# Seven products per group: three of them accumulate in one bank, two banks are copied into banks, and two sums between banks stand where there were four

## The chip, the cores and the metric

The kernel runs on one core of a Trainium2 chip. Five engines work side by side, each through its own queue in order: TensorE (PE, matrix products; PEld is its loading of the stationary operand), VectorE (DVE), ScalarE (ACT), GpSimd (POOL) and SyncE (SP, which here only issues transfers). Products are written to banks of PSUM; one bank holds 128 rows of 512 float32 numbers. The metric is the time of the whole program on the device in microseconds (us), as the median of the runs; smaller is better.

## The reference

One decoder block on 256 rows of width 2048 in float32. The two feed-forward parts, which the change touches, are these:

```
h = h + 0.5 * swiglu(rms_norm(h, ffn1_norm), ffn1_w_gu, ffn1_w_down)
h = h + hybrid_mixer(rms_norm(h, mix_norm), ...)
h = h + 0.5 * swiglu(rms_norm(h, ffn2_norm), ffn2_w_gu, ffn2_w_down)
gate = sigmoid(rms_norm(h, ple_norm) @ ple_w_gate)
h = h + gate * (p @ ple_w_proj)
return rms_norm(h, final_norm)

def swiglu(x, w_gu, w_down):
    gate, up = split(x @ w_gu, 2)          # 2048 -> 2 x 5632
    return (silu(gate) * up) @ w_down      # 5632 -> 2048
```

## The kernel before

**Precision.** Each float32 operand is split into a rounded part and a rest (`hi` and `lo`, for weights `whi`/`wlo`, for activations `nTh`/`nTl` and `hTh`/`hTl`), and each product is three matmuls: hi·hi, hi·lo, lo·hi. ACT makes the rounded part of a weight (line 74), DVE the rest (line 75). A weight pair is 256 rows of a weight by 512 columns; for both halves of the 256 rows of x it takes 12 matmuls of 128x512.

**Groups.** A feed-forward part is a list of groups (`Group`, line 245). A group makes 256 rows by two blocks of 512 columns, so it owns four banks: c11 and c21 (first block of columns, rows 0 to 127 and 128 to 255) and c12 and c22 (second block). In the profile they carry the names g, g, u, u in a group of the gate and up product and d, d, d, d in a group of the down product. Groups take turns between two pools of four banks. `PARTS` cuts the 11 blocks of the hidden width into parts of 3, 4 and 4: the gate and up groups of a part come first, then its two down groups.

**Seven products.** A share of each group's depth (`ns` pairs of each block; 4 for gate and up, 2 or 3 for down) is not multiplied plainly in eight block products but in seven, in the manner of Strassen and Winograd: sums of blocks of the activations (`halves`, lines 420 to 462: `S`, split into `Sh` and `Sl`) are multiplied with sums of blocks of the weights (`all_sums`, lines 287 to 322: `R`, split by ACT into `shi`, line 295, and by DVE into `slo`, line 296). `product(i)` (line 324) issues product i: 3·ns matmuls, so 12, 9 or 6. There are 32 such groups, 15 in the first feed-forward part, 16 in the second and one behind it, so 224 products. The first one or two groups of a feed-forward part have no such products, and the first group that has them is marked `first`.

Before the change product 0 goes to c11, 1 to c12, 2 to c21, 3 to c22. After product 2, `add` (line 338) adds c11 to c21 and subtracts c21 from c12; after product 3 it subtracts c22 from c21 and adds c12 to c22. Each `add` is an ACT copy of one bank to a buffer in SBUF (`part`, line 341) and a DVE sum of the other bank with it (line 342). Products 4, 5 and 6 are accumulated on c11, c12 and c21.

**Order.** `plan` (line 351) strews the seven products of the next group between the plain pairs of the current one, one product behind each pair, from the second or third pair on; where the pairs run out, two products stand side by side. `next_weights` (line 82) loads and splits weights up to two pairs and one sum ahead. The code is written in that order, but a scheduler in the layer below sets the final order of each engine's queue: it may move an instruction past others on its engine. So the place of a product, a copy or a sum in its queue is read from the built program, not from the code.

Twice in the kernel a down group needs the hidden values of the gate and up group just ahead of it. They travel from DVE through DRAM back to a tile `tT` and are split by ACT (line 499, `hTh`) and DVE (line 500, `hTl`).

Of the kernel before, what the change touches and what calls it, by code (L numbers as in the profile page):

```python
# [13 lines left out]
ALU = mybir.AluOpType  # L14
# [29 lines left out]
def block_kernel(ctx, tc, a, out):  # L44
    nc = tc.nc
# [18 lines left out]
    def weight_pair(src, pool=wp, bufs=3, parts=1):  # L64

        raw = wp.tile([P, 2, NB], F32, tag="raw", name="raw", bufs=4)
        hi = pool.tile([P, 2, NB], F32R, tag="whi", name="whi", bufs=bufs)
        lo = pool.tile([P, 2, NB], F32R, tag="wlo", name="wlo", bufs=bufs)
        for i in range(parts):
            j = slice(2 * i // parts, 2 * (i + 1) // parts)  # L70
            nc.sync.dma_start(out=raw[:, j, :], in_=src[:, j, :])
        for i in range(parts):
            j = slice(2 * i // parts, 2 * (i + 1) // parts)
            nc.scalar.copy(hi[:, j, :], raw[:, j, :])  # L74
            nc.vector.tensor_tensor(out=lo[:, j, :], in0=raw[:, j, :], in1=hi[:, j, :], op=ALU.subtract)  # L75
        return hi, lo
# [5 lines left out]
    def next_weights():  # L82

        ahead = max(1, min(LEAD, done[1] // 2))
        while done[0] < len(order):
            kind, src = order[done[0]]
            if kind != "load" and sum(k == kind for k, _ in split) > (ahead if kind == "pair" else 1):
                break
            done[0] += 1
            if kind == "load":  # L90
                src()
            elif kind == "sum":
                split.append((kind, next(src.sums)))
            else:
                split.append((kind, weight_pair(src, parts=2 if not done[1] and not split else 1)))
        done[1] += 1
        return split.pop(0)[1]
# [145 lines left out]
    current, sides = [None], {}  # L243

    class Group:
# [78 lines left out]
        def product(self, i):  # L324

            if i == 0:
                self.new_banks()
            c11, c21, c12, c22 = self.banks
            out = (c11, c12, c21, c22, c11, c12, c21)[i]
            whi, wlo = next_weights()  # L330
            for g in range(self.ns):
                xh, xl = sides[self.kind](i, g)
                st, sp = i < 4 and g == 0, i < 4 and g == self.ns - 1
                nc.tensor.matmul(out, xh, whi[:, g, :], start=st, stop=False, skip_group_check=True)  # L334
                nc.tensor.matmul(out, xh, wlo[:, g, :], start=False, stop=False, skip_group_check=True)  # L335
                nc.tensor.matmul(out, xl, whi[:, g, :], start=False, stop=sp, skip_group_check=True)  # L336

            def add(out, x, op):

                part = act.tile([P, NB], F32, tag="nat", name="part", bufs=4)  # L340
                nc.scalar.copy(part, x)
                nc.vector.tensor_tensor(out=out, in0=out, in1=part, op=op)

            if i == 2:
                add(c21, c11, ALU.add)
                add(c12, c21, ALU.subtract)
            elif i == 3:
                add(c21, c22, ALU.subtract)
                add(c22, c12, ALU.add)

    def plan(n):

# [67 lines left out]
    def halves(kind, his, los, ns, wait=0):  # L420


        for _ in range(wait):
            yield
        fp = current[0]

        sh = fp.tile([P, NS, 2, 2, P], F32R, tag="Sh", name="Sh")
        sl = fp.tile([P, NS, 2, 2, P], F32R, tag="Sl", name="Sl")

        def side(i, g):  # L430
            if i in (0, 4, 6):
                k, t = 2 * (g % 2) + (i > 0), i // 6
                c = slice(t * P, (t + 1) * P)
                return his[g // 2][:, k, c], los[g // 2][:, k, c]
            j, t = {1: (1, 1), 2: (0, 0), 3: (0, 1), 5: (1, 0)}[i]
            return sh[:, g, j, t, :], sl[:, g, j, t, :]

        sides[kind] = side

        for g0 in range(0, ns, 2):  # L440
            n = min(2, ns - g0)
            hi, lo = his[g0 // 2], los[g0 // 2]
            keep = lambda ins: ins
            if g0 and n == 1:

                keep = tc.keep_in_program_order
                yield
            if n == 2:
                x = fp.tile([P, 2 * NB], F32, tag="sil", name="S")
            else:  # L450
                x = act.tile([P, NB], F32, tag="nat", name="S", bufs=4)
            keep(nc.vector.tensor_tensor(out=x, in0=hi[:, 0:2 * n].bitcast(F32).rearrange("p k x -> p (k x)"),
                                         in1=lo[:, 0:2 * n].bitcast(F32).rearrange("p k x -> p (k x)"), op=ALU.add))
            xv = x.rearrange("p (g j t y) -> p g j t y", g=n, j=2, t=2)
            a11, a12, a21, a22 = (xv[:, :, j, t, :] for t in range(2) for j in range(2))
            for o, y, z, op in ((a22, a21, a22, ALU.subtract), (a21, a21, a11, ALU.subtract),
                                (a11, a22, a11, ALU.subtract), (a12, a11, a12, ALU.add)):
                nc.vector.tensor_tensor(out=o, in0=y, in1=z, op=op)
            sx = [y[:, g0:g0 + n].rearrange("p g j t y -> p (g j t y)") for y in (sh, sl)]
            nc.scalar.copy(sx[0], x)  # L460
            nc.vector.tensor_tensor(out=sx[1], in0=x, in1=sx[0], op=ALU.subtract)
            yield

    def ffn(n, nT, r, scale, next_norm, stat):
        xs = picker(*nT)
        late = callable(r)
        with tc.tile_pool(name="ffn", bufs=1) as fp:
# [40 lines left out]
            nxt = None  # L508
            current[0] = fp
            lanes.add(1, halves("gu", *nT, NS, 6 if late else 0))  # L510
            for group, todo in ffn_plan[n]:
                if group.kind == "behind":
# [4 lines left out]
                if dn and group.nb and not group.last:  # L517
                    lanes.add(1, halves("gu", *nT, NS))
                elif dn and group.nb and group.follower:
                    lanes.add(1, halves("behind", *nxt, NS_BEHIND, 4))  # L520
                elif not dn and group.follower.kind == "dn":
                    lanes.add(1, halves("dn", hTh[i0:], hTl[i0:], NS_DOWN[group.part]))
# [116 lines left out]
    with tc.tile_pool(name="fin", bufs=1) as fp:  # L639
# [35 lines left out]
        for _, (nb, g) in todo:  # L675
            whi, wlo = next_weights()
            for j in range(2):
                k = 2 * g + j
                xh, xl = xs(k)
                for t in range(2):  # L680
                    c = slice(t * P, (t + 1) * P)
                    gt, sp = group.banks[2 * nb + t], k == KD - 1
# [695 lines left out]
```

## Time and profile before

| | |
|---|---|
| median of 3 runs | 1946.12 us (1945.83 to 1947.10) |
| the profiled execution: span from its first to its last instruction | 1944.1 us |
| PE busy, TensorE clock granted | 99% of the span, 0.999 |
| DVE, ACT, POOL busy | 82%, 60%, 8% |
| mean of a product's ACT copy and DVE sum (lines 341, 342) | 0.584 to 0.591 us, 0.693 to 0.696 us |
| first feed-forward part, mixer, second part | to about 690 us, to about 1155 us, to about 1850 us |

The median lies 2.0 us above the span of the profiled execution. In the rows below, a row of the timeline is: start, length, engine, line, operation, output from input, number of instructions merged in the row, and in brackets the idle time of the engine just before it with what ended that. A row of the windows is: the stretch, its length, and for PE, PEld, DVE, ACT and POOL the busy time with the number of instructions in brackets, then the granted TensorE clock, the busy share of the DMA engines and GB/s. A matmul's row is longer than its place in the pipeline: what counts is the distance between two starts.

### The profile page before, as it was taken

To read this page: it belongs to the slowest core of one execution; us is meant where nothing else is said; L and a number is where in the kernel's file an instruction comes from. 1 tells how busy PE (TensorE), PEld (TensorE's weight loads), DVE (VectorE), ACT (ScalarE), POOL (GpSimd) and SP (SyncE) were. 2 spreads that over 40 slices of the span, in tenths; PEclk is the share of its full clock that TensorE was granted. 3 is DMA by queue.
4 is the path that set the end of the run, shared out by engine and by line. 5 is a ranking of instruction groups with operands and counts; after the bars stand their busy time and mean duration, and the time that the engine had idled before them with its cause. 6 is when DMAs were issued, how large, how long until landed. Compare 5 with 4: busy or idle time off the path is not lost.

```text
span 1944.1 us, 24295 instructions
## 1 busy us (share of the span) xinstructions
PE 1927.9 (99%) x8882; PEld 1593.1 (82%) x8882; DVE 1603.2 (82%) x1743; ACT 1163.4 (60%) x1358; POOL 148.8 (8%) x226
## 2 busy tenths in 40 slices
PE   9999999999999999999999999999999999999998
PEld 7888888888888888878788888888888888888887
DVE  7879988998889866797856679899888998889965
ACT  6655656566665567654555456566565755657654
POOL 0010110000001000010100000011000100001000
PEclk9999999999999999999999999999999999999999
DMA  8778898898898765556464776788898988989864
GB/s 306 269 217 291 256 292 272 248 296 247 269 288 255 224 218 171 173 167 218 159 215 157 243 278 229 236 268 285 260 278 253 306 257 261 264 263 273 253 212 147
DMA packets 144183, 475.06 MB, mean 244 GB/s; under 512 B 19648, under 2 KB 47296, under 8 KB 129856
## 3 DMA queue, kind: packets, MB, share of 16 engines
q1 hardware_dynamic: 104896, 293.78, 43.6%
q0 software_dynamic: 25920, 160.44, 29.9%
q10 hardware_dynamic: 13248, 19.30, 3.3%
q8 instruction: 69, 1.13, 0.2%
q14 instruction: 50, 0.41, 0.1%
HBM read 451.44 MB, written 22.02 MB: 244 GB/s over the span
## 4 chain that ended last, share of the span: by engine, by line
PE 91%; DVE 6%; issue 1%; DMA 1%; ACT 1%; POOL 0%; SPq 0%; POOLq 0%; DVEq 0%; ACTq 0%
PE d L540 5%; PE d L541 5%; PE d L542 5%; PE u L541 5%; PE u L542 5%; PE u L540 5%; PE g L541 4%; PE g L542 4%; PE pj L109 4%; PE pj L110 4%; PE pj L111 4%; PE g L540 4%; PE g L335 4%; PE g L334 4%; PE g L336 4%; PE u L334 3%
## 5 line engine op out<-in xcount | busy, mean ns | idle before, releaser
L74 ACT CAST whi<-raw 128x1024 fp32r<-128x1024 f32 (+1 forms) x489 | 511.7, 1050 | 420.0 <-PE pj L111 108.9
L75 DVE TENSOR_TENSOR wlo<-raw,whi 128x1024 fp32r<-128x1024 f32 (+1 forms) x489 | 590.8, 1217 | 155.8 <-ACT whi L74 153.1
L296 DVE TENSOR_TENSOR slo<-R,shi 128x2048 fp32r<-128x2048 f32 (+2 forms) x224 | 444.4, 1987 | 99.9 <-ACT shi L295 99.7
L295 ACT CAST shi<-R 128x2048 fp32r<-128x2048 f32 (+2 forms) x224 | 374.0, 1673 | 185.6 <-DVE R L304 74.4
L109 PE MATMUL pj<-whi,nTh 128*128 128x512 f32 x448 | 179.4, 401 | 0.0
L110 PE MATMUL pj<-wlo,nTh 128*128 128x512 f32 x448 | 175.3, 391 | 1.4 <-DVE wlo L75 1.4
L111 PE MATMUL pj<-whi,nTl 128*128 128x512 f32 x448 | 174.9, 390 | 0.0
L541 PE MATMUL d<-wlo,hTh 128*128 128x512 f32 x448 | 174.4, 389 | 0.0
L542 PE MATMUL d<-whi,hTl 128*128 128x512 f32 x448 | 174.0, 389 | 0.0
L540 PE MATMUL d<-whi,hTh 128*128 128x512 f32 x448 | 173.1, 390 | 0.0
L541 PE MATMUL g<-wlo,nTh 128*128 128x512 f32 x400 | 156.1, 390 | 0.6 <-DVE wlo L75 0.6
L540 PE MATMUL g<-whi,nTh 128*128 128x512 f32 x400 | 154.9, 390 | 1.2 <-ACT whi L74 0.9
L542 PE MATMUL g<-whi,nTl 128*128 128x512 f32 x400 | 155.9, 390 | 0.0
L541 PE MATMUL u<-wlo,nTh 128*128 128x512 f32 x400 | 155.7, 389 | 0.1
L542 PE MATMUL u<-whi,nTl 128*128 128x512 f32 x400 | 155.6, 389 | 0.0
L540 PE MATMUL u<-whi,nTh 128*128 128x512 f32 x400 | 154.2, 389 | 0.0
L304 DVE TENSOR_TENSOR R<-R 128x2048 f32<-128x2048 f32 (+2 forms) x68 | 135.4, 1991 | 0.1
L110 PEld LDWEIGHTS pj<-wlo,nTh 128*128 128x128 f32 x448 | 84.2, 188 | 19.2 <-DVE wlo L75 3.0
L540 PEld LDWEIGHTS d<-whi,hTh 128*128 128x128 f32 x448 | 84.1, 188 | 17.9 <-ACT hTh L499 0.7
L542 PEld LDWEIGHTS d<-whi,hTl 128*128 128x128 f32 x448 | 84.1, 188 | 17.7
L111 PEld LDWEIGHTS pj<-whi,nTl 128*128 128x128 f32 x448 | 84.1, 188 | 17.5
L541 PEld LDWEIGHTS d<-wlo,hTh 128*128 128x128 f32 x448 | 84.1, 188 | 17.4
(327 smaller groups left out, 3482.5 us busy)
## 6 DMA issues: line engine op xcount, KB each, us to landing
raw<-in_w_gu SPq DMA_DIRECT2D x199, 512.0 KB, 5.7
raw<-in_w_down SPq DMA_DIRECT2D x112, 512.0 KB, 6.4
raw<-in_w_in SPq DMA_DIRECT2D x112, 512.0 KB, 3.4
R<-in_w_gu2q POOLq DMA_DIRECT2D x54, 1024.0 KB, 8.1
R<-in_w_gu1q POOLq DMA_DIRECT2D x48, 1024.0 KB, 8.7
raw<-in_w_out SPq DMA_DIRECT2D x32, 512.0 KB, 4.4
R<-in_w_down11q POOLq DMA_DIRECT2D x12, 768.0 KB, 6.8
R<-in_w_down12q POOLq DMA_DIRECT2D x12, 768.0 KB, 6.3
```

The source lines that it names most:

```text
L74: nc.scalar.copy(hi[:, j, :], raw[:, j, :])
L75: nc.vector.tensor_tensor(out=lo[:, j, :], in0=raw[:, j, :], in1=hi[:, j, :], op=ALU.subtract)
L109: nc.tensor.matmul(outs[t], xh[:, c], whi[:, j, :], start=st, stop=False)
L110: nc.tensor.matmul(outs[t], xh[:, c], wlo[:, j, :], start=False, stop=False)
L111: nc.tensor.matmul(outs[t], xl[:, c], whi[:, j, :], start=False, stop=sp)
L295: keep(nc.scalar.copy(hi, w))
L296: nc.vector.tensor_tensor(out=lo, in0=w, in1=hi, op=ALU.subtract)
L304: keep(nc.vector.tensor_tensor(out=self.raw[x], in0=self.raw[x], in1=self.raw[y], op=ALU.add))
L334: nc.tensor.matmul(out, xh, whi[:, g, :], start=st, stop=False, skip_group_check=True)
L540: nc.tensor.matmul(out, xh[:, c], whi[:, j, :], start=st, stop=False, skip_group_check=True)
L541: nc.tensor.matmul(out, xh[:, c], wlo[:, j, :], start=False, stop=False, skip_group_check=True)
L542: nc.tensor.matmul(out, xl[:, c], whi[:, j, :], start=False, stop=sp, skip_group_check=True)
```

## The change

```
-            out = (c11, c12, c21, c22, c11, c12, c21)[i]
+            out = (c21, c12, c21, c21, c11, c12, c21)[i]
             whi, wlo = next_weights()
+            if i == 0 and self.first == "2":
+
+                for x in (c11, c22):
+                    nc.tensor.matmul(x, sides[self.kind](0, 0)[0], whi[:, 0, :], start=True, stop=True,
+                                     skip_group_check=True)
             for g in range(self.ns):
                 xh, xl = sides[self.kind](i, g)
-                st, sp = i < 4 and g == 0, i < 4 and g == self.ns - 1
+                st, sp = i < 2 and g == 0, i < 4 and g == self.ns - 1
...
-            def add(out, x, op):
-
+            if i < 2:
+                nc.scalar.copy((c11, c22)[i], out)
+            elif i < 4:
                 part = act.tile([P, NB], F32, tag="nat", name="part", bufs=4)
-                nc.scalar.copy(part, x)
-                nc.vector.tensor_tensor(out=out, in0=out, in1=part, op=op)
-
-            if i == 2:
-                add(c21, c11, ALU.add)
-                add(c12, c21, ALU.subtract)
-            elif i == 3:
-                add(c21, c22, ALU.subtract)
-                add(c22, c12, ALU.add)
+                nc.scalar.copy(part, c21)
+                x = (c12, c22)[i - 2]
+                nc.vector.tensor_tensor(out=x, in0=x, in1=part, op=ALU.subtract)
...
-            for o, y, z, op in ((a22, a21, a22, ALU.subtract), (a21, a21, a11, ALU.subtract),
+            for o, y, z, op in ((a22, a21, a22, ALU.subtract), (a21, a11, a21, ALU.subtract),
```

Product 0 now goes to c21, and ACT copies c21 into the bank c11; product 1 goes to c12 as before, and ACT copies it into the bank c22. Products 2 and 3 are accumulated on c21 by PE itself; after each of them ACT copies c21 to `part`, and DVE subtracts that from c12 after product 2 and from c22 after product 3. One sum of the activations changes its sign. So each group keeps four ACT copies, of which two now write a bank, and has two DVE sums in place of four. In the first such group of the second feed-forward part, two matmuls on c11 and c22 are added. The lines behind the change move down by five: `shi`, `slo` and the sums keep theirs, the products' matmuls are lines 339 to 341 (334 to 336 before), the copies between banks line 344, the copies to `part` line 347, and the sums line 349.

The queues move with it at a few places. In the rows below, the operand names carry the buffer numbers, which differ between the two programs; the first bank in the list of a group is c11, then c21, c12, c22.

On PE, in the first seven-product group of the first feed-forward part (banks g0_722, g1_723, u0_724, u1_725), where the last matmul of product 0 stands between plain matmuls of the group ahead. Before:

```order
L336 MATMUL g0_722<-shi_660,nTl_104 128x512
L334 MATMUL u0_724<-shi_684,Sh_295 128x512
L335 MATMUL u0_724<-slo_685,Sh_295 128x512
L336 MATMUL u0_724<-shi_684,Sl_296 128x512
L541 MATMUL g0_524<-wlo_579,nTh_101 128x512
```

The same place now:

```order
L341 MATMUL g1_723<-shi_660,nTl_104 128x512
L541 MATMUL g0_524<-wlo_579,nTh_101 128x512
L542 MATMUL g0_524<-whi_578,nTl_105 128x512
L541 MATMUL g1_525<-wlo_579,nTh_101 128x512
L542 MATMUL g1_525<-whi_578,nTl_105 128x512
```

Before, three matmuls of product 1 stood here, and its other nine (three, then six) among the next plain pairs; now all twelve stand behind six plain pairs, 70 matmuls further on, and the plain matmuls that need the weight rests `wlo_579`, and a pair later `wlo_597`, move up by three and by six places.

On PE, in the second down group behind the first three hidden blocks of the first feed-forward part (banks d0_1315, d1_1316, d0_1317, d1_1318 before; d0_1307, d1_1308, d0_1309, d1_1310 now), at products 2 and 3, just ahead of the plain matmuls that need the late hidden values `hTh_1238` (now `hTh_1230`). Before:

```order
L334 MATMUL d1_1316<-shi_1325,Sh_1012 128x512
L334 MATMUL d1_1318<-shi_1354,Sh_1012 128x512
L335 MATMUL d1_1316<-slo_1326,Sh_1012 128x512
L336 MATMUL d1_1316<-shi_1325,Sl_1013 128x512
L334 MATMUL d1_1316<-shi_1325,Sh_1012 128x512
L335 MATMUL d1_1316<-slo_1326,Sh_1012 128x512
L336 MATMUL d1_1316<-shi_1325,Sl_1013 128x512
L335 MATMUL d1_1318<-slo_1355,Sh_1012 128x512
```

Now:

```order
L339 MATMUL d1_1308<-shi_1318,Sh_1008 128x512
L340 MATMUL d1_1308<-slo_1319,Sh_1008 128x512
L341 MATMUL d1_1308<-shi_1318,Sl_1009 128x512
L339 MATMUL d1_1308<-shi_1318,Sh_1008 128x512
L340 MATMUL d1_1308<-slo_1319,Sh_1008 128x512
L341 MATMUL d1_1308<-shi_1318,Sl_1009 128x512
L339 MATMUL d1_1308<-shi_1348,Sh_1008 128x512
L340 MATMUL d1_1308<-slo_1349,Sh_1008 128x512
```

Products 2 and 3 went to two banks (c21 and c22) and were interleaved; now product 3 follows product 2 in one bank with no matmul between. The mirror of this group in the second feed-forward part stands in the same way.

On ACT at that same place. Before:

```order
L295 CAST shi_1325<-R_1150 128x1024
L295 CAST shi_1354<-R_1208 128x1024
L74 CAST whi_1399<-raw_1398 128x1024
L295 CAST shi_1392<-R_1218 128x1024
L499 CAST hTh_1238<-tT_1310 128x4x4x32 x2
L341 COPY part_1389<-d1_1316 128x512
```

Now:

```order
L295 CAST shi_1318<-R_1145 128x1024
L344 COPY d1_1310<-d0_1309 128x512
L295 CAST shi_1348<-R_1200 128x1024
L74 CAST whi_1390<-raw_1389 128x1024
L347 COPY part_1380<-d1_1308 128x512
L295 CAST shi_1383<-R_1210 128x1024
L499 CAST hTh_1230<-tT_1302 128x4x4x32 x2
```

The copy between banks (after product 1) and the copy of product 2 now stand ahead of the weight sum of product 4 (`shi_1383`) and of the split of the hidden values. The mixer between the two feed-forward parts has the same rows in the same order on every engine.

## The prediction, made before the changed kernel was run

> **What bounds the kernel now.** I read the page's busy times and its chain of work first.
>
> ```profile
> PE 1927.9 (99%) x8882; PEld 1593.1 (82%) x8882; DVE 1603.2 (82%) x1743; ACT 1163.4 (60%) x1358; POOL 148.8 (8%) x226
> ...
> PE 91%; DVE 6%; issue 1%; DMA 1%; ACT 1%; POOL 0%; SPq 0%; POOLq 0%; DVEq 0%; ACTq 0%
> ```
>
> PE carries the chain. DVE, where the change takes work away, holds 6% of it: short spells in which PE stands ready for something that DVE has just finished. How long PE really stood there is in the waits of PE (total us, times, longest):
>
> ```profile
> PE pj L110 <- DVE wlo L75: 1.4, 3, 0.6
> PE vp L1109 <- DVE R L1130: 1.2, 1, 1.2
> ...
> PE d L335 <- DVE slo L296: 0.6, 2, 0.3
> PE u L335 <- DVE slo L296: 0.3, 1, 0.3
> ```
>
> The longest belong to the mixer, which the change leaves alone. In the feed-forward parts they are fractions of a microsecond. But a matmul's row overlaps the next, so a stall is longer than the idle time shown; it is the starts that count. The windows show where starts are missing:
>
> ```profile
> 50.00:100.00 50.00, 49.30 (x217) 40.07 (x216) 43.49 (x34) 31.09 (x31) 1.30 (x2) 1.00 0.74 267
> 150.00:200.00 50.00, 49.70 (x216) 40.00 (x216) 49.23 (x52) 30.83 (x31) 5.74 (x8) 1.00 0.87 278
> 250.00:300.00 50.00, 50.00 (x222) 41.38 (x222) 40.52 (x29) 31.20 (x27) 5.05 (x8) 1.00 0.89 285
> 1300.00:1350.00 50.00, 49.70 (x216) 39.81 (x215) 48.85 (x49) 31.44 (x31) 5.34 (x8) 1.00 0.90 290
> ```
>
> Undisturbed, PE starts 222 matmuls in 50 us, one each 0.225 us, at the full granted clock (1.00). It lacks 5 in the stretch from 50 us and 6 each in those from 150 and 1300 us. These three stretches are the stalls that the change can take away or make longer; the last two are also where DVE is busy 98% of the time.
>
> **The change part by part.**
>
> Removed: half of the DVE sums. The copies and sums of before, by line (count, then shortest, median and longest in ns):
>
> ```profile
> L341 ACT COPY part<-d x48: 567/583/599, 131.3 to 1791.7; 128x512 f32<-128x512 f32 x48
> L341 ACT COPY part<-g x40: 569/588/593, 82.1 to 1833.7; 128x512 f32<-128x512 f32 x40
> L341 ACT COPY part<-u x40: 589/591/602, 96.3 to 1837.3; 128x512 f32<-128x512 f32 x40
> ```
>
> ```profile
> L342 DVE TENSOR_TENSOR d<-d,part x48: 689/693/700, 133.1 to 1792.3; 128x512 f32<-128x512 f32 x48
> L342 DVE TENSOR_TENSOR g<-g,part x40: 691/693/700, 91.0 to 1838.2; 128x512 f32<-128x512 f32 x40
> L342 DVE TENSOR_TENSOR u<-u,part x40: 687/690/700, 95.0 to 1838.8; 128x512 f32<-128x512 f32 x40
> ```
>
> There are 128 of each, four in each of 32 groups. 64 sums of 0.69 us go, 44 us of DVE's 1603. As PE is busy 99%, this is worth only what it takes off PE's stalls; elsewhere DVE idles longer.
>
> Changed in kind: 64 of the 128 ACT copies now write a bank. The trace has no ACT write to a bank. Of ACT's rows that read a bank and write a buffer, the nearest is the copy itself, 0.584 us; an activation of the same shape is slower and one of half its width the shortest of that kind:
>
> ```profile
> L505 ACT ACTIVATE sil<-g,rstd 128x512 f32<-128x512 f32 x44 | 28.9, 687 | 10.5 <-DVE Sl L461 8.5 <-PE g L542 1.5
> ...
> L936 ACT ACTIVATE cT<-tr_p,conv 128x256 f32<-128x256 f32 x24 | 10.2, 470 | 9.0 <-DVE cT L938 9.0
> ```
>
> I bound it by 0.47 and 0.69 us and take 0.58. Between the two bounds, 64 copies differ by 14 us on an engine that idles 780. The next matmul that touches a copied bank is product 2 on c21 and product 4 on c11, with at least a plain pair and product 1 between (24 matmuls, 5.4 us), so either bound costs nothing on PE.
>
> Added: two matmuls in the second part, straight onto PE: 2 x 0.225 = **+0.45 us**.
>
> Moved: product 1 in the first group of the first part. Here are PE and then DVE at that place before:
>
> ```profile
> 65.11 0.39 PE L336 MATMUL g<-shi,nTl 128*128 128x512 f32 x1
> 65.34 0.40 PE L334 MATMUL u<-shi,Sh 128*128 128x512 f32 x1
> 66.04 0.50 PE L335 MATMUL u<-slo,Sh 128*128 128x512 f32 x1 [0.30 <-DVE slo L296]
> 66.38 0.39 PE L336 MATMUL u<-shi,Sl 128*128 128x512 f32 x1
> 67.17 0.50 PE L541 MATMUL g<-wlo,nTh 128*128 128x512 f32 x1 [0.40 <-DVE wlo L75]
> 67.51 0.40 PE L542 MATMUL g<-whi,nTl 128*128 128x512 f32 x1
> ```
>
> ```profile
> 63.70 2.29 DVE L296 TENSOR_TENSOR slo<-R,shi 128x2048 fp32r<-128x2048 f32 x1
> 65.90 1.22 DVE L75 TENSOR_TENSOR wlo<-raw,whi 128x1024 fp32r<-128x1024 f32 x1
> 67.04 2.29 DVE L304 TENSOR_TENSOR R<-R 128x2048 f32<-128x2048 f32 x1
> 69.24 3.49 DVE L75 TENSOR_TENSOR wlo<-raw,whi 128x1024 fp32r<-128x1024 f32 x3
> ```
>
> PE waits twice: for `slo` (0.47 us late, then 0.11 until it is back in step) and for `wlo` (0.57 and 0.11), 1.26 in all. The three matmuls of product 1 that filled part of the gap are now gone from it, and DVE's order here is unchanged, since the first sums that the change removes come at 91 us. So the plain matmul due at 65.34 waits until 67.17 for the same `wlo`: 1.83 + 0.11. The next plain pair follows after 12 matmuls rather than 15: due at 67.51 + 11 x 0.225 = 69.99, while its `wlo`, the first of the three from 69.24, is ready at 70.46 and usable some 0.05 later (as 67.17 follows 67.12): 0.52 + 0.11. Together 2.57, so **+1.31 us**. Before, that pair was due three matmuls later, at 67.51 + 14 x 0.225 = 70.66, and did not wait. The two `wlo` after that are ready at 71.6 and 72.8, ahead of need. Product 1 itself moves 16 us down, where its `slo` is long ready; nothing is won there, since it waited only as filler.
>
> A new wait: product 3 now needs c21, and so the ACT copy behind product 2. Queued behind it on PE are plain matmuls; on ACT, behind the copy that waits for PE, the next `shi` and `whi`. From the start of product 2's last matmul: 0.39 for its row, 0.58 for the copy, and about 0.05 for each hand-over, 1.07 us. In nearly all groups a plain pair of 12 matmuls stands between, so PE asks after 13 x 0.225 = 2.93 us: 1.9 us to spare. At three places only four matmuls stand between (1.13 us): nothing, or a tenth. At two places, in the second down group behind the first three hidden blocks of each feed-forward part, none stands between: 1.07 - 0.23, and 0.11 to get back in step, **0.95 us**. But both lie in the stalls at 160 and 1300 us:
>
> ```profile
> 160.01 0.61 PE L334 MATMUL d<-shi,Sh 128*128 128x512 f32 x2
> 160.21 1.05 ACT L74 CAST whi<-raw 128x1024 fp32r<-128x1024 f32 x1 [0.67 <-PE d L542]
> 160.91 0.50 PE L335 MATMUL d<-slo,Sh 128*128 128x512 f32 x1 [0.29 <-DVE slo L296]
> ...
> 162.38 1.05 ACT L295 CAST shi<-R 128x1024 fp32r<-128x1024 f32 x1 [1.12 <-PE d L336]
> ...
> 163.10 0.39 PE L336 MATMUL d<-shi,Sl 128*128 128x512 f32 x1
> 163.34 1.14 ACT L499 CAST hTh<-tT 128x512 fp32r<-128x512 f32 x2
> 163.49 0.50 PE L334 MATMUL d<-shi,hTh 128*128 128x512 f32 x1
> ...
> 164.00 0.50 PE L540 MATMUL d<-whi,hTh 128*128 128x512 f32 x1
> ```
>
> Before, PE lost 0.45 + 0.11 to DVE's `slo` at 160.91, then 0.16 to ACT's `shi` at 163.49, 0.28 to `hTh` at 164.00, and 0.11: 1.11 us. Now there are two ends. If the two sums that DVE no longer makes in the group ahead (1.4 us) bring `slo` forward by half a microsecond or more, product 2 runs from 160.01, its sixth matmul starts at 161.14, product 3 starts at 162.20 and the matmul on `hTh` at 163.89, in step: 0.2 won. If `slo` comes when it came before, product 2's sixth starts at 161.93, product 3 at 163.0 and the matmul on `hTh` at 164.68: 0.6 lost. I take the middle, +0.2 at each place, **+0.4 us**, with ends of -0.4 and +1.2.
>
> **Sum.** 0.45 + 1.31 + 0.4 = +2.2 us on the profiled span: 1944.1 to 1946.3. The median of the runs lies 2.0 above that span, so I forecast 1946.1 + 2.2 = **1948.3 us**. This is +0.11%, within the 0.2% (3.9 us: 1942.2 to 1950.0) that a measurement of this kernel can tell from no change.
>
> **Rivals.**
>
> *The freed DVE wins.* DVE runs ahead also where I take the middle or where I hold its order fixed, so that the stalls at 160 and 1300 us vanish whole (2 x 1.11) and only the first group's loss stays: 0.45 + 1.31 - 2.22 = -0.5, 1945.7. For it: DVE is 98% busy there. Against it: the copy between products 2 and 3 is new at just these places, and `hTh` stands behind it on ACT. If the first group lost nothing either, it would be 1944.3. Even with all the stalls of the rows above gone (1.26 + 2.22) the sum would be 0.45 - 3.48 = -3.0, 1943.1: a gain that can be measured is nearly shut out.
>
> *The order is not what decides.* The first group's loss does not come, because the matmuls that moved up are met by an earlier `wlo`; then 0.45 + 0.4, 1947.0. Against it: DVE's rows there are the same.
>
> *Slower: ACT comes late to the copy behind product 2.* ACT works in order and now stops at each copy until PE has ended the product, so casts pile up behind and ahead of the copies. From ACT's groups and its waits before:
>
> ```profile
> L295 ACT CAST shi<-R 128x2048 fp32r<-128x2048 f32 (+2 forms) x224 | 374.0, 1673 | 185.6 <-DVE R L304 74.4 <-PE u L336 38.8 <-PE g L336 23.5
> ```
>
> ```profile
> ACT part L341 <- PE u L336: 28.9, 19, 2.1
> ```
>
> If a `shi` cast (mean 1.67 us) and a `whi` cast (1.05, the row at 160.21) still stand ahead of the copy when the product ends, it comes 2.72 us late. That is 0.86 more than the 1.86 to spare (2.93 - 1.07), and with 0.11 to get back in step 0.97 us for PE. It decides from a copy that starts 1.86 us late. In a third of the 27 ordinary groups that is 8.7 us, 1957; in all of them 26 us, 1974. Against it: ACT idles 40%, and before such copies it used to stand and wait (the row: 19 times, up to 2.1 us).
>
> The Trainium skill, PSUM — Partial Sum Buffer, "Summary: rules for kernel authors", takes this side: PSUM is to be read in a different bank than a running matmul writes, with a guard for each bank. By that rule alone, with no work between, product 3 would lose the 0.95 us in all 32 groups, 30 us, and the time would be 1977. The order of the changed program speaks against that, since plain matmuls on other banks stand between in 30 of the 32; no run shows it yet.
>
> **How the numbers follow.** Forecast 0.60 (own range 1946.5 to 1950); freed DVE 0.12; order not deciding 0.11; ACT late 0.13; something that takes off more than the stalls I can see, 0.04. Faster by over 0.2% is the last, 0.04. Slower by over 0.2% is the ACT case and the forecast's upper end, 0.13 + 0.07 = 0.20. The rest, 0.76, is the same. The range runs from 1944.5, below the freed DVE's 1945.7, to 1952.5, which takes in both late ends and an ACT loss in four or five groups (4 us) and leaves out the larger ones.
>
> **What would show each step.** The DVE sums down to 64 and DVE's busy time by some 44 us; ACT copies into banks near 0.58 us. At 65 us, PE held some 1.8 us by `wlo` and again some 0.5 us at 70 us. Near 161 and 1304 us, product 3's first matmul held by the ACT copy of c21, about 0.95 us. No wait of PE for ACT's `part` in the other groups. The forecast is wrong if PE waits for `part` all over the feed-forward parts, or if its count of starts in steady stretches leaves 222 in 50 us.

## The result, and the profile after

| kernel | runs | median us | lowest to highest | span of the profiled execution |
|---|---|---|---|---|
| before | 4 | 1946.61 | 1945.83 to 1947.52 | 1944.1 |
| after | 4 | 1954.57 | 1953.82 to 1956.19 | 1952.5 |

The ratio is 1.0043, 95% interval 1.0029 to 1.0057. The change costs about 8 us. The forecast was 1948.3 with a range to 1952.5, and "slower by over 0.2%" had a chance of 0.20: the prediction was wrong, and the upper end of its range was too low.

From the page after, the engines' busy time and the chain by engine:

```profile
PE 1930.7 (99%) x8884; PEld 1594.0 (82%) x8884; DVE 1569.4 (80%) x1679; ACT 1164.3 (60%) x1358; POOL 148.4 (8%) x226
...
PE 88%; DVE 6%; DMA 3%; ACT 1%; issue 1%; POOL 0%; SPq 0%; ACTq 0%; POOLq 0%; DVEq 0%
```

DVE has 64 instructions fewer and PE two more, as the change says. In the chain DMA has 3% where it had 1%. The windows after, in the prediction's three stretches and in four others (columns: window; its length, then PE's busy time and starts, PEld, DVE, ACT, POOL; granted clock, DMA share, GB/s):

```profile
50.00:100.00 50.00, 48.10 (x211) 39.01 (x210) 41.70 (x32) 30.20 (x30) 1.30 (x2) 1.00 0.71 259
150.00:200.00 50.00, 49.32 (x217) 40.28 (x217) 48.51 (x49) 31.17 (x32) 5.72 (x8) 1.00 0.87 276
350.00:400.00 50.00, 48.53 (x213) 39.54 (x212) 45.38 (x47) 30.65 (x33) 4.98 (x8) 1.00 0.85 262
600.00:650.00 50.00, 48.96 (x215) 39.86 (x214) 44.12 (x45) 32.63 (x36) 4.83 (x7) 1.00 0.87 263
1300.00:1350.00 50.00, 49.32 (x218) 40.33 (x217) 48.23 (x48) 32.09 (x33) 4.78 (x7) 1.00 0.91 278
1500.00:1550.00 50.00, 49.08 (x216) 39.83 (x215) 45.53 (x48) 32.78 (x36) 5.35 (x8) 1.00 0.87 263
1750.00:1800.00 50.00, 48.75 (x214) 39.73 (x213) 44.87 (x45) 34.71 (x37) 5.88 (x9) 1.00 0.88 262
```

Count the starts, at 0.225 us each. From 50 us PE has 211 where it had 217: 1.35 us lost, the predicted term. From 150 and 1300 us it has one and two more than before: a little won. The four others are the news. Each of them had 222 starts before, no stall at all, and now lacks 9, 7, 6 and 8: 30 starts, **6.8 us**. PE's waits name what it stood for (total us, times, longest):

```profile
PE d L339 <- ACT Sh L460: 3.4, 4, 1.1
PE g L541 <- DVE wlo L75: 1.9, 2, 1.6
PE d L339 <- ACT part L347: 1.4, 2, 0.7
PE d L341 <- DVE Sl L461: 1.3, 4, 0.3
```

The second and third rows were forecast: two waits for `wlo` in the first group, two for the copy of c21 between products 2 and 3. The first and the last are the four new places: the first down group of each part with four hidden blocks, at its product 1, which reads `Sh` and `Sl`, the sums of the hidden values.

**Back along the wait, at 358 us.** ACT and PE after, from the timeline (start, duration, engine, line; in brackets the idle time before and what ended it):

```profile
356.51 0.31 ACTq L492 DMA_DIRECT2D tT<-scr  x1
356.86 0.57 ACT L344 COPY d<-d 128x512 f32<-128x512 f32 x1 [4.30 <-DMA scr<-tb]
...
357.35 1.48 ACT L295 CAST shi<-R 128x1536 fp32r<-128x1536 f32 x1
...
358.72 1.05 ACT L460 CAST Sh<-S 128x1024 fp32r<-128x1024 f32 x1
```

```profile
359.82 0.50 PE L339 MATMUL d<-shi,Sh 128*128 128x512 f32 x1 [1.14 <-ACT Sh L460]
```

Before, ACT came to the same `Sh` at 356.11 and waited there for DVE's `S` alone:

```profile
356.11 1.06 ACT L460 CAST Sh<-S 128x1024 fp32r<-128x1024 f32 x1 [1.21 <-DVE S L458]
```

ACT idles 4.30 us and then does the copy, `shi` and `Sh` in a row. The copy between banks is not what it waits for: product 0 had ended by 353.5. Ahead of the copy on ACT's queue stands the issue of `tT<-scr`, the transfer that brings the transposed hidden block back, and that waits until `scr<-tb`, the store of the same block, has landed. Before, the issue of two of these loads was at 350.80, not at 356.51. So the store is late. The timeline has its issue and that of the transfer beside it, the accumulating load of `R` that POOL issues (L311); the list of DMA issues has the store's size and the us from issue to landing. Before:

```profile
347.10 0.89 POOL L311 DMA_DIRECT2D R<-in_w_down11q  x1 [9.95 <-DVE R L304]
347.45 0.34 ACTq L487 DMA_DIRECT2D scr<-tb  x1
```

```profile
scr<-tb ACTq DMA_DIRECT2D x1, 512.0 KB, 3.3
```

And after:

```profile
346.99 0.89 POOL L311 DMA_DIRECT2D R<-in_w_down11q  x1 [8.98 <-DVE R L304]
347.94 0.34 ACTq L487 DMA_DIRECT2D scr<-tb  x1
```

```profile
scr<-tb ACTq DMA_DIRECT2D x1, 512.0 KB, 8.6
```

The store goes out 0.95 us behind the load, where it went out 0.35 us behind it, and takes 8.6 us rather than 3.3. The reason for those 0.6 us is on DVE. Before, and after:

```profile
342.78 1.75 DVE L296 TENSOR_TENSOR slo<-R,shi 128x1536 fp32r<-128x1536 f32 x1
344.45 0.70 DVE L482 STREAM_TRANSPOSE tb<-sil 128x512 f32<-128x512 f32 x1
345.08 1.72 DVE L304 TENSOR_TENSOR R<-R 128x1536 f32<-128x1536 f32 x1
346.72 0.70 DVE L482 STREAM_TRANSPOSE tb<-sil 128x512 f32<-128x512 f32 x1
```

```profile
344.94 1.75 DVE L304 TENSOR_TENSOR R<-R 128x1536 f32<-128x1536 f32 x1
346.60 1.30 DVE L482 STREAM_TRANSPOSE tb<-sil 128x512 f32<-128x512 f32 x2
```

The load waits for the sum into `R`, the store for both transposes. With two sums fewer in the group ahead and product 3 behind a copy, the scheduler put that `slo` earlier (at 339.60) and the sum into `R` ahead of both transposes. Before, only one transpose came between the two releases; now two do. The other three places show the same, with landings of 8.1, 8.0 and 8.0 us for 3.3, 3.3 and 2.6.

### The profile page after: what moved, and what is told of

The parts are those of the page before. It is cut to its first block, busy times and chain, and to the rows that moved or that the text cites. A ratio compares the mean times of both kernels' runs of the same rounds, so it can differ in the third digit from the quotient of the medians.

```text
span 1952.5 us, 24206 instructions
## 1 busy us (share of the span) xinstructions
PE 1930.7 (99%) x8884; PEld 1594.0 (82%) x8884; DVE 1569.4 (80%) x1679; ACT 1164.3 (60%) x1358; POOL 148.4 (8%) x226
## 4 chain that ended last, share of the span: by engine, by line
PE 88%; DVE 6%; DMA 3%; ACT 1%; issue 1%; POOL 0%; SPq 0%; ACTq 0%; POOLq 0%; DVEq 0%
PE d L542 5%; PE d L540 5%; PE d L541 5%; PE g L340 4%; PE g L339 4%; PE g L341 4%; PE u L541 4%; PE u L542 4%; PE u L540 4%; PE pj L109 4%; PE pj L110 4%; PE pj L111 4%; PE g L541 4%; PE g L542 3%; PE g L540 3%; PE d L341 3%
```

## The experiments

**Theory A**, read from these rows: the changed groups shift DVE's order, the store falls in behind the accumulating load, ACT stands at the issue of `tT`, and `Sh` and `Sl` are late. **Rival B**: the new copies into banks stand ahead of `Sh` on ACT and make it late by themselves. In the kernels below line numbers are a few higher than in the changed kernel. Each ratio is to the kernel before as it ran beside these runs, with a median of 1946.15 us for runs 1 to 4, 1946.29 for 5 to 8 and 1945.88 for 9 and 10.

**1. Move the load, nothing else.** The load is issued with product 1 rather than product 0, and waits for that product's `slo` (`self.low`):

```diff
-                nc.gpsimd.dma_start(out=self.raw[x], in_=self.quarters[y[1]][y[0]], accum_op=ALU.add)
+                load = nc.gpsimd.dma_start(out=self.raw[x], in_=self.quarters[y[1]][y[0]], accum_op=ALU.add)
+                if late_load and x == (0, 1):
+                    tc.add_manual_dep(load.ins, self.low.ins.name, mybir.DependencyInfo(
+                        mybir.DependencyClass.Sync, mybir.DependencyReason.DATA), reason="late load")
...
+            late_load = self.kind == "dn" and self.nb == 0 and self.ns == 3
...
```

> The changed kernel, with one wait added in four places: the accumulating load of R that POOL issues just ahead of the store scr (first down group of each part with four hidden blocks) waits for the next slo on DVE, some 4 us later. The order of every engine's instructions is that of the changed kernel. Theory A (the store scr falls in behind this load on the DMA engines and lands after 8 us where it took 3; ACT stands at the issue of tT<-scr, and the cast Sh behind it is late for product 1): the store lands in about 3 us again, PE's 3.4 us of waits for Sh go, and the four stalls of 1.5 to 2.0 us with them: 6.9 us off 1954.6, 1947.7, with 0.7 to either side. Rival B (the new ACT copies into banks, which stand ahead of Sh on ACT, make it late): nothing changes, 1954.6. Rival C (the load is needed soon, so that moving it back makes slo of product 3 late): the stalls move from product 1 to product 3, 1951 or more.

Measured 1946.81 us, ratio to before 1.0004 (0.9995 to 1.0012), clear of the changed kernel's 1.0029 to 1.0057. At the first of the places, from the timeline, the DMA issues and the windows:

```profile
347.60 0.34 ACTq L494 DMA_DIRECT2D scr<-tb  x1
...
351.77 0.89 POOL L311 DMA_DIRECT2D R<-in_w_down11q  x1 [14.10 <-DVE slo L296]
```

```profile
scr<-tb ACTq DMA_DIRECT2D x1, 512.0 KB, 2.7
```

```profile
350.00:400.00 50.00, 50.00 (x222) 41.28 (x221) 46.97 (x49) 32.72 (x36) 6.29 (x9) 1.00 0.91 265
```

The load goes out 4 us behind the store, which lands in 2.7 us, and PE has its 222 starts again. In the other three places it has 221, 222 and 222. All 64 copies into banks are still there. Rival B falls, and so does C, since the later load makes nothing else late.

**2. The same wait in the kernel before**, as a control.

> The kernel before, with the same wait on the same four loads: a control. Theory A: the store was ahead of the load there already (3.3 us to landing), so nothing is won; 1946.6, with 0.6 to either side. If the later load gained or cost something by itself, it would show here as more than 1 us.

1945.56 us, ratio 0.9999 (0.9990 to 1.0008). The later load by itself is worth nothing; what it mends is the order of the two.

**3. The late store in the kernel before.** The first hunk takes down the sum into `R`, the second puts both transposes behind it:

```diff
+                if self.kind == "dn" and self.nb == 0 and self.ns == 3 and x == (0, 0) and y == (0, 1):
+                    behind.append(ins.ins)
...
-                    nc.vector.transpose(tb[:, :, t].rearrange("p c (j x) -> p c j x", j=4),
-                                        sil[:, t, :].rearrange("p (j c x) -> p c j x", j=4, c=4))
+                    with tc.issue_after(behind[-1]) if behind else ExitStack():
+                        nc.vector.transpose(tb[:, :, t].rearrange("p c (j x) -> p c j x", j=4),
+                                            sil[:, t, :].rearrange("p (j c x) -> p c j x", j=4, c=4))
```

> The kernel before, all 128 sums and no copies into banks, with one thing of the changed kernel's order: in the same four places both transposes tb stand behind the sum into R on DVE, as the change has them, rather than one on each side of it. Theory A: the store goes out 0.6 us later, falls in behind the load, takes 6 to 9 us, and PE loses at Sh and Sl in four places: 1951 to 1954. Rival B (ACT's copies into banks): no loss, 1946.6, with 0.6 to either side.

1956.98 us, ratio 1.0056 (1.0043 to 1.0069): the whole loss and more, with no copy between banks in the kernel. The timeline at the first place, and PE's wait over the whole span:

```profile
346.94 0.89 POOL L314 DMA_DIRECT2D R<-in_w_down11q  x1 [9.49 <-DVE R L304]
347.89 0.34 ACTq L492 DMA_DIRECT2D scr<-tb  x1
```

```profile
PE d L337 <- ACT Sh L463: 2.7, 4, 0.9
```

The gap of 0.95 us is that of the changed kernel, and the store took 8.0 us. The run lost 47 starts in the four windows, 10.6 us, more than the 5 to 8 that I expected: the pin also moved instructions behind it, and PE waited for `wlo` too in these places.

**4. Take `tT` off ACT's queue**, in the four places alone (`third`):

```diff
-                    keep(queue.dma_start(out=tT[32 * c:32 * c + 32].rearrange("x q t i -> x q (t i)"),
+                    keep((nc.gpsimd if third else queue).dma_start(out=tT[32 * c:32 * c + 32].rearrange("x q t i -> x q (t i)"),
...
```

> The changed kernel, with the four loads tT<-scr of the third hidden block (four places) issued by POOL rather than by ACT, so that ACT does not stand at them. Theory A, second link: the store still takes about 8 us, but ACT's copy, shi and Sh no longer wait for it; the four stalls go, 1947.7 with 1.5 to either side (the order of some instructions behind shifts with it). If ACT's stand is not what makes Sh late, the stalls stay: 1954.6.

1950.29 us, ratio 1.0022 (1.0013 to 1.0031): half of the way. The store still took 8.2 us at the first place, and no wait of PE for `Sh` is left, so the second link holds. But 14 of the 30 starts are still missing. POOL issues the `tT` loads in order behind its next load of `R`, at 359.69, later than ACT had done, and at this place PE now waits 0.8 us for a `shi`. The expectation took POOL's queue for free; it wasn't.

**5. The sums of before in four of the 32 groups**, those whose sums run just ahead of the four places. The last hunk has two more sums, with the copies into `part` as before:

```diff
+                groups[-1].own_banks = i - i0 == 3
...
+            out = ((c11, c12, c21, c22) if self.own_banks else (c21, c12, c21, c21))[i] if i < 4 else (c11, c12, c21)[i - 4]
...
+            if self.own_banks:
+                if i == 2:
+                    add(c21, c11, ALU.add)
+                    add(c12, c21, ALU.subtract)
...
```

> The changed kernel, with four of its 32 groups (the last gate-and-up group of each part with four hidden blocks) computed as before: a bank for each of products 0 to 3, four copies into a buffer and four sums. With this the order on DVE at the third hidden block of these parts is that of before again: slo, a transpose, the sum into R, a transpose. No wait is added. Theory A (the changed groups ahead shift DVE's order, and that puts the store behind the load): the store lands in about 3 us and the time is that of the run with the later load, 1946.8, with 1 to either side. Rival B (ACT's copies into banks, which the down groups keep): 1954, with 1 to either side.

1948.43 us, ratio 1.0011 (1.0003 to 1.0020), 0.6 above the expected band and 1.6 above run 1. The places themselves are mended: 222, 221, 222 and 221 starts, and the store landed in 3.3 us again, 0.36 us behind the load. So the shift on DVE does come from the changed groups ahead. Where the 1.6 us went I did not follow.

**6. The smallest mend: the load waits for the transpose that the store waits for.** As run 1, with the wait on the last transpose (`turned[-1]`):

```diff
-                    tc.add_manual_dep(load.ins, self.low.ins.name, mybir.DependencyInfo(
+                    tc.add_manual_dep(load.ins, turned[-1], mybir.DependencyInfo(
```

> The changed kernel, with the accumulating load of R in the four places waiting only for the second transpose tb, the one that the store waits for too: POOL and ACT then issue at about the same moment, and the load is some 1 us later than in the changed kernel. Every engine's order is that of the changed kernel. POOL's issue took 0.9 us and ACT's 0.34, so the store should reach the DMA engines first: about 3 us to landing, and 1946.8, with 0.7 to either side, as with the load that was moved 4 us. If the two still share the engines from the start, the store takes 5 us or more and part of the stalls stay: 1949 to 1953.

1947.27 us, ratio 1.0005 (0.9996 to 1.0014). POOL issued at 347.65, 0.27 us behind ACT's 347.38, and the store took 2.6 us. With the rows above this makes a scale: the store lands in 2.6 to 3.3 us when it goes out 4 us ahead of the load to 0.36 us behind it, and in 8.0 to 8.7 us when it goes out 0.7 to 0.95 us behind it. What turns over between the two is which issue ends first. POOL takes 0.89 us to issue the load and ACT 0.34 us to issue the store: at 0.35 us behind, the store's issue ended at 347.79 and the load's at 347.99; at 0.95 us behind, the load's ended at 347.88, before the store's began. In all four places of every run the store is quick where its issue ended first and slow where the load's did.

**7 and 8. The first group, by DVE's order.** The predicted loss there, 1.3 us, was put down to `slo` standing ahead of `wlo` on DVE. Here `shi` and `slo` of that group stay in program order (7 also has the later load of run 1):

```diff
-                keep(nc.scalar.copy(hi, w))
+                (tc.keep_in_program_order if self.first else (lambda x: x))(nc.scalar.copy(hi, w))
...
+                if self.first == "1":
+                    tc.keep_in_program_order(self.low)
```

> The changed kernel with the later load and, in the first seven-product group of the first part, shi and slo kept in program order on ACT and DVE, behind the wlo of the plain pairs, so that product 0 runs in its place and does not go ahead of them. If the two waits of PE for wlo at 65 and 70 us come from the slo that stand ahead of them on DVE (2.5 us of PE in the changed kernel), they go: 1946.8 - 2.5 = 1944.3, with 0.8 to either side. If products 0 and 1 have no other cover further down, new waits for slo at 80 to 95 us take their place, and it stays at 1946 to 1947.

> The kernel before with the same order of shi and slo in that first group, and nothing else: it lost 1.26 us there. If those waits go, 1946.2 - 1.3 = 1944.9, with 0.8 to either side; with the run above it shows what the change itself is worth where the order costs nothing on either side: the predicted 0.45 for the two matmuls and about 0.4 for the wait of product 3, less what freed DVE.

1950.25 us, ratio 1.0020 (1.0011 to 1.0029), and 1949.74, ratio 1.0018 (1.0009 to 1.0027): 5 to 6 us above what was expected, and slower than the kernel before. Run 7, ACT and PE from the timeline, then a window:

```profile
63.78 1.04 ACT L74 CAST whi<-raw 128x1024 fp32r<-128x1024 f32 x1 [8.00 <-DMA raw<-in_w_gu]
...
64.88 0.73 PE L549 MATMUL g<-whi,nTh 128*128 128x512 f32 x2 [2.03 <-ACT whi L74]
...
68.01 0.63 PE L549 MATMUL g<-whi,nTh 128*128 128x512 f32 x1
68.44 0.63 PE L550 MATMUL g<-wlo,nTh 128*128 128x512 f32 x1
```

```profile
67.50:70.00 2.50, 2.50 (x7) 1.93 (x6) 1.22 (x1) 0.72 (x1) 0.00 (x0) 0.50 1.00 298
```

The two profiles are 0.9 us apart here, so I count from the last plain matmul ahead of this place, which starts at 61.53 in the changed kernel and at 62.46 in run 7. `wlo` starts 4.0 us behind it in the changed kernel (65.53) and 2.4 us behind it in run 7 (64.86), so the `slo` ahead of it on DVE did hold it back, by 1.6 us. But the edit holds back product 0 as well, which in the changed kernel runs right behind that matmul, from 61.76. It had been the cover for the load of `raw`: without it ACT stood 8 us for that load and PE 2.03 us, after which its clock was at 0.50 and a matmul took 0.427 us to the next, until 72.3.

**9 and 10. The first group, by the loads.** From 50 to 65 us the DMA engines are fully busy, and four loads of `R`, 1 MB each, stand together ahead of `raw` on SP's queue.

```diff
-                    loads.setdefault(max(at[0] - 5, 0), []).extend(follower.loads())
+                    for x, one in zip((0, 1, 3, 5) if n == "1" else (at[0] - 5,) * 4, follower.loads()):
+                        loads.setdefault(x, []).append(one)
```

> The changed kernel with the accumulating load behind the second transpose (as in the run before) and, in the first part, the four first loads of R, 1 MB each on SP's queue, issued with the plain pairs 0, 1, 3 and 5 of the group ahead, rather than all four at pair 3. If PE's waits for wlo at 65 and 70 us (2.5 us of PE) come from the raw loads that stand behind these 4 MB on SP's queue and on the DMA engines (their share was 1.0 from 50 to 65 us), they go: 1947.3 - 2.5 = 1944.8, with 0.8 to either side. If DVE's slo ahead of wlo are the cause, as the prediction had it, the waits stay: 1946.5 to 1947.5.

> The kernel before with the same four loads of R spread over the pairs 0, 1, 3 and 5. It lost 1.26 us at 65 us: if the loads are the cause, 1946.2 - 1.3 = 1944.9, with 0.8 to either side; if DVE's order is, 1946 to 1946.5. With the run above: what the change is worth where neither the store nor these loads cost PE anything; the predicted 0.45 for the two matmuls and 0.4 for product 3's wait say 0.5 to 1 us slower.

1944.97 us, ratio 0.9995 (0.9986 to 1.0003), and 1944.56, ratio 0.9994 (0.9985 to 1.0003). Run 9 at the place:

```profile
60.00:65.00 5.00, 5.00 (x24) 4.14 (x23) 5.00 (x4) 4.01 (x4) 0.00 (x0) 1.00 0.76 278
65.00:70.00 5.00, 5.00 (x24) 4.14 (x23) 5.00 (x4) 1.06 (x1) 0.00 (x0) 1.00 0.72 221
```

Both have 222 starts in the 50 us from 50, where before had 217 and after 211, and no wait of PE is left there. So spreading the loads takes the waits away. It doesn't take `slo` from its place ahead of `wlo`. DVE in the changed kernel, then in run 9:

```profile
55.49 2.25 DVE L296 TENSOR_TENSOR slo<-R,shi 128x2048 fp32r<-128x2048 f32 x1
...
63.33 2.29 DVE L296 TENSOR_TENSOR slo<-R,shi 128x2048 fp32r<-128x2048 f32 x1
65.53 1.22 DVE L75 TENSOR_TENSOR wlo<-raw,whi 128x1024 fp32r<-128x1024 f32 x1
```

```profile
48.72 2.29 DVE L296 TENSOR_TENSOR slo<-R,shi 128x2048 fp32r<-128x2048 f32 x1 [0.58 <-ACT shi L295]
...
61.36 2.29 DVE L296 TENSOR_TENSOR slo<-R,shi 128x2048 fp32r<-128x2048 f32 x1
63.56 2.35 DVE L75 TENSOR_TENSOR wlo<-raw,whi 128x1024 fp32r<-128x1024 f32 x2
```

In the changed kernel DVE idles 0.03 us in all from 55.49 to 65.53, and `whi` was ready at 64.19, 1.3 us before `wlo` began: DVE's backlog held `wlo`, not `raw`. In run 9 the first of the loads goes out at 38.50 rather than 45.64, so the first `slo` runs at 48.72, where DVE used to idle, and everything behind it comes 2 us earlier. `raw` lands earlier too (a median of 4.4 us for 7.9 between 46 and 72 us); no run moves one without the other. Run 9, the changed kernel with both mends, is clear of the changed kernel; against the kernel before it reads 1 us faster, but its interval holds 1, as that of run 10 does. Between run 9 and run 10, 0.4 us of median: the change itself is worth nothing that these runs can tell.

## Why the prediction was wrong

- **"This is worth only what it takes off PE's stalls; elsewhere DVE idles longer."** This is the step that failed. It costed the removed DVE work at nothing or a gain wherever PE had no stall. But fewer sums also move what is left on DVE, and in four places the order of two releases turned over: the sum that lets POOL's load go, and the transposes that let ACT's store go. Those 0.6 us became 5 us in the landing of the store and 6.8 us on PE, of the 8.4 us that the span grew. Runs 1, 3 and 5 show it from three sides. The wait that came of it, ACT at the issue of a load that needs the store, stood in none of the sum's terms.
- **The two added matmuls**, +0.45: 8884 rows for 8882. Too small for the runs to show alone.
- **The first group**, +1.31: right in size, 6 starts or 1.35 us, and PE waited 1.6 and 0.3 us for `wlo` (by the starts 1.76 and 0.48), near the 1.83 and 0.52 forecast. The reason held as well: product 1, moved down, left the wait uncovered, and `wlo` was late because `slo` stood ahead of it on DVE, by 1.6 us (run 7). What the prediction didn't ask is why DVE was so far behind there: the four loads of `R` came late and together, and with them spread the loss goes (runs 9 and 10).
- **Product 3 behind the copy of c21**: at the two narrow places PE stood 0.7 us each for `part`, as forecast, and the old stalls there went; the counts say 0.2 to 0.4 us won at each, the favourable end of the -0.4 to +1.2 given for both, not the middle.
- **The copies into banks** took less than I took them for, and cost PE nothing:

```profile
L344 ACT COPY d<-d x24: 570/570/582, 126.7 to 1789.2; 128x512 f32<-128x512 f32 x24
```

- **Rival, ACT late to the copy behind product 2.** It had the right engine and a near time, 1957, for a wrong reason. In the ordinary groups PE never waited for `part`: all such waits are the two of the narrow places. The 30 us that the prediction worked out for a wait in every group did not come either: ACT read and wrote banks in 32 groups beside matmuls on others, and PE waited for the copy in two of them, 0.7 us each. The Trainium skill, PSUM — Partial Sum Buffer, "Summary: rules for kernel authors", has PSUM read in another bank than the one that a running matmul writes. The trace agrees: only these two, with no work on other banks between, paid.
- **Rival, the freed DVE wins**: the stalls on `slo` at 160 and 1304 us did go, but the wait for `part` took most of their place.
- **The range** stopped at 1952.5 because every slower case was worked out as a wait on PE, DVE or ACT. None was on a transfer, though a store 0.35 us behind a load of 768 KB stood in the profile before, with nothing to hold that order.

## What to carry to other kernels

When a change moves instructions, look past the compute rows to what each of them releases: a sum or a transpose that lets a transfer go is also a place in the DMA engines' queue, and two transfers released within a microsecond of each other can change places. Where one of them is waited for soon, write that order down (run 6 needed one wait) rather than leave it to what happens to end first. And before mending a wait, look at what is behind the instruction that is waited for: in runs 7 and 8 the obvious cure took away the cover of a later load.

## What the runs showed of the hardware

**The store waited until the load was nearly through.** Packets by queue in one microsecond (packets, MB, share of 16 engines), first the kernel before from 348 us, where q10 carries the store, then the changed kernel from 351 us, where q0 carries the load that was issued 0.95 us ahead of it:

```profile
q10 hardware_dynamic: 67, 0.27, 74.6%
```

```profile
q0 software_dynamic: 33, 0.20, 100.2%
q10 hardware_dynamic: 1, 0.00, 1.1%
```

Whichever had its issue end first had the engines nearly to itself; the store, issued at 347.94, had moved one packet by 352. Later in the same kernel, from 354 us, the store and the loads on SP's queue (q1) did share them evenly:

```profile
q1 hardware_dynamic: 52, 0.21, 51.9%
q10 hardware_dynamic: 50, 0.20, 49.7%
```

The Trainium skill, DMA: Bandwidth & Descriptors, "Queues, rings and completion order", says that each DMA engine takes turns between the queues it has work for, packet by packet. The rows from 354 us agree with it. By that rule, as an estimate, the store would have had about half of the engines from the start; the rows from 351 us don't show that, so there the measurement decides. What inside the engines kept the store back, no run here shows.

**PE's clock fell after 2 us of standing.** In run 7 a wait of 2.03 us (2.42 us between two starts) had another of 0.52 us close behind it. The granted clock then read 0.50 from about 65.5 to 72.3, and a start came each 0.427 us. In run 8, after 2.17 and 0.53 us, it was 0.50 from about 64.5 to 68. In the changed kernel a wait of 1.6 us (1.98 us between starts), with one of 0.3 us some 3 us later, left the clock at 1.00. The Trainium skill, TensorE: Matmul & The Clock Gate, "Why this matters for your kernels", advises against idle gaps over about 3 us; in these runs 2.0 us and half a microsecond more were enough.
